# Two feed-forward networks by seven products: a fourth pair in the down panels, x kept in DRAM, its blocks added by accumulating DMAs

## The chip, the core and the metric

The kernel runs on one core of one Trainium2 chip, as one program. Its time is the device time of one execution, in microseconds; the median of three runs before the change is 2627.86 us (2625.54 to 2630.56). Five engines work side by side, each through its own list of instructions in a fixed order, and wait for each other at semaphores: TensorE (PE) multiplies, VectorE (DVE) and ScalarE (ACT) do the arithmetic on elements, GpSimd (POOL) and SyncE (SP) here mostly start DMAs.

## What is computed

Two transformer layers on 256 tokens of width 2048 in float32, each a mixer (state space or gated delta rule beside sparse attention) and a feed-forward network. The change touches the feed-forward networks and what hands x to them. Each is, after an RMS norm whose row factor is applied later,

```
u = rmsnorm(x, g_mlp) @ w_up          # [256, 2048] @ [2048, 8192]
x = x + jnp.square(jax.nn.relu(u)) @ w_down   # [256, 8192] @ [8192, 2048]
```

## The kernel before

Every number is split in two parts, hi (`whi`, `xnh`, `hTh`) and lo (`wlo`, `xnl`, `hTl`), and a product of two blocks is three matmuls: hi by hi, hi by lo, lo by hi. ACT copies a stretch of weights to `whi` (line 266 in the wide panels, 207 in the others), and DVE subtracts it from the weights for `wlo` (lines 267, 208). These have four buffers of 1024 columns each; a buffer is free again when PE has used it.

A network (`ffn`) goes in four steps (`s_`) of 2048 hidden columns. A step is four wide panels, called here U0 and U1 (two up panels, which make the hidden block) and D0 and D1 (two down panels, which add to x). A wide panel multiplies 256 tokens by 2048 rows and 1024 columns of weights; it goes through eight pairs, `j` from 0 to 7, of 256 rows. A pair is a 2 by 2 block problem: two token blocks, two halves of the rows, two halves of the columns. A plain pair takes eight products, 24 matmuls. For the pairs in `SPAIRS`, 2, 4 and 6, a seven-product scheme is used, 21 matmuls. It wants sums of the weight blocks, `t13` (line 284) and `t24` (287 and 288, after `t13`), all on DVE, then four splits: `w11` with `w22` straight from the weights, `t13`, `t24`, and a half one of the last block. It also wants sums of the activations, made once per pair (`a_forms`, lines 232 to 235, and a split, `sfh` on ACT and `sfl` on DVE).

After a wide panel, `shared` combines four banks of the accumulators (ACT copies P1 at 311, DVE adds at 312 to 315). After an up panel each of the four results gets its own bank added (DVE, 381), then ReLU and square on ACT (382, 383), then 16 transposes on PE (395), then a split to `hTh` and `hTl` (170, 172), and the sums for the pairs in `SPAIRS`, through a tile `ff`. All this is done while the next wide panel runs. After a down panel, the four results and the four banks are added to x in SBUF by eight DVE instructions (415, 418). The last down panel of a network is done by `panel` (plain products, lines 192 to 194).

The weights come in through SP's queue, 1 MB per pair, into three buffers `wst`; a load is started when DVE has made the last split of the pair three before. Large tiles share pools: seven `sp` (four of them hold x during a network, so three are left for `t13` and `t24`), seventeen `s4`, sixteen `s2`. The order of each engine's instructions is fixed at build time by a list scheduler, which goes by its own estimate of when things are ready and which prefers what stands earlier in the program.

Of the kernel before, what the change touches and what calls it, by code (L numbers as in the profile page):

```python
# [57 lines left out]
def build(ctx, tc, I, out, tap=None, upto=99):  # L58
# [162 lines left out]
    SPAIRS = (2, 4, 6)  # L221
    turn = [0]

    def two_forms():
        f = s4([128, 2, 512], name="ff")
        return f[:, 0].rearrange("p (k t c) -> p k t c", k=2, t=2), f[:, 1].rearrange("p (f c) -> p f c", f=4)
# [13 lines left out]
    def wide(w, r0, c0, lhs, forms):  # L240
# [8 lines left out]
        ns = len(SPAIRS)  # L249
# [20 lines left out]
        for j in range(8):  # L270
# [3 lines left out]
            if j not in SPAIRS:  # L274
                for kk in range(2):
                    xh, xl = lhs(2 * j + kk)
                    wl = parts(s[:, kk * 1024:(kk + 1) * 1024])[::-1]
                    for i, l, b in ((0, 0, "P2"), (0, 1, "P3"), (1, 0, "P4"), (1, 1, "E")):
                        h = slice(i * 128, i * 128 + 128)
                        product(b, xh[:, h], xl[:, h], *wl[l])  # L280
                continue
# [26 lines left out]
    def shared(B):  # L308

        p1, u2, u4, v = (s2([128, 512], name=n) for n in ("cp1", "cu2", "cu4", "cv"))  # L310
# [5 lines left out]
        return ((0, 0, p1, B["P2"]), (0, 1, u4, B["P3"]), (1, 0, u2, B["P4"]), (1, 1, v, B["E"]))  # L316
# [57 lines left out]
    def ffn(X, act, forms, w_up, w_down, r, after, tail=0):  # L374
        for s_ in range(4):
            hT, hforms = [], {}
            for P in range(2):
                B, tags = wide(w_up, 0, s_ * 2048 + P * 1024, at_k(act), forms)
                us = {}
                for i, l, part, bank in shared(B):  # L380
# [4 lines left out]
                for l in (1, 0):  # L385
# [3 lines left out]
                    for k0 in range(0, 4, 2):  # L389
# [7 lines left out]
                        if j in SPAIRS:  # L397
# [5 lines left out]
            for P in range(2):  # L403
                if (s_, P) == (3, 1):
# [7 lines left out]
                out_ = shared(B)  # L412
                for i, l, part, bank in out_:
                    x = X[2 * P + 1 - l][:, i]
                    V.tensor_tensor(x, part, x, op=OP.add)
                for i, l, part, bank in out_:
                    x = X[2 * P + 1 - l][:, i]
                    V.tensor_tensor(x, bank, x, op=OP.add)
                if s_ == 3:
                    for p in range(2):  # L420
# [369 lines left out]
    def add_panel(ps, p, scale, act, gain, ssx, forms):  # L790
# [5 lines left out]
        for t in range(2):  # L796
            sumsq(ssx[:, t, p:p + 1], X[p][:, t])

    X = x_panels()
# [20 lines left out]
    ffn(X, xn, xforms, I["w_up"][0], I["w_down"][0], r, after1)  # L820
# [513 lines left out]
    xforms = {}  # L1334
    ssx = tiny([128, 2, 4], "ssx", bufs=2)
    for p in range(4):
# [6 lines left out]
        for t in range(2):  # L1343
            sumsq(ssx[:, t, p:p + 1], X[p][:, t])
    r = x_rstd(ssx, "r4")
# [27 lines left out]
    ffn(X, xn, xforms, I["w_up_2"][0], I["w_down_2"][0], r, after2, tail=8)  # L1373
# [23 lines left out]
```

## Time and profile before

| | |
|---|---|
| median of 3 runs | 2627.86 us |
| profiled execution, whole | 2628.55 us |
| its span, first to last instruction | 2626.7 us |
| PE busy | 2600.1 us, 99% |
| weight loads of PE (PEld) busy | 2173.6 us, 83% |
| DVE busy | 2037.6 us, 78% |
| ACT busy | 1466.7 us, 56% |
| DMA | 478.64 MB, 182 GB/s |

The profile is one execution; times in it are microseconds from the span's start. Busy time is the union of an engine's instructions. A DVE or ACT instruction runs on a little after the next has begun, so in a row of instructions the price of one is the distance of two starts, a little less than its duration. A line such as L267 is a line of the kernel before; in the changed kernel it is the same line up to 286, and one to eleven later further down.

### The profile page before, as it was taken

Reading aid. Unit: us, or ns where it says so; the run is one execution under the profiler, and the core shown is the slowest. Engines: PE = TensorE matmul, PEld = TensorE weight load, DVE = VectorE, ACT = ScalarE, POOL = GpSimd, SP = SyncE. Lnnn points to the kernel's source line nnn. Section 1 sums busy time; section 2 is a strip of 40 time slices with the busy share of each in tenths; the row PEclk is TensorE's granted clock in tenths of the full one; section 3 lists DMA queues with packets and bytes.
Section 4 is the critical chain, followed back from the end, with each engine's and each line's share of the span. In section 5 each row is a group of like instructions: output and inputs, shape, how many; then the busy total and the mean of one; then the engine's idle time right before and its main releaser. Section 6 shows DMA issues by size and latency. Waiting matters only on the chain.

```text
span 2626.7 us, 32683 instructions
## 1 busy us (share of the span) xinstructions
PE 2600.1 (99%) x12566; PEld 2173.6 (83%) x12566; DVE 2037.6 (78%) x2797; ACT 1466.7 (56%) x1962; POOL 37.5 (1%) x46
## 2 busy tenths in 40 slices
PE   8999999999999999999999999999999999999998
PEld 8998888888888888888888887888888888888886
DVE  5767768998989999676755867455579999999996
ACT  5465456646657566554533655444457566565664
POOL 0000000000000000000000000000000000000000
PEclk9999999999999999999999999999999999999999
DMA  7454555565655655653432743556555655555654
GB/s 239 143 177 155 170 192 192 177 207 193 193 198 187 208 193 196 203 189 129 132 98 87 260 165 111 180 189 211 197 176 179 218 196 197 193 204 192 208 181 172
DMA packets 192154, 478.64 MB, mean 182 GB/s; under 512 B 9127, under 2 KB 50046, under 8 KB 191998
## 3 DMA queue, kind: packets, MB, share of 16 engines
q1 hardware_dynamic: 185840, 467.57, 53.7%
q10 hardware_dynamic: 6158, 8.99, 1.1%
q8 instruction: 98, 1.61, 0.2%
q14 instruction: 58, 0.48, 0.1%
HBM read 472.32 MB, written 4.21 MB: 181 GB/s over the span
## 4 chain that ended last, share of the span: by engine, by line
PE 90%; DVE 6%; DMA 2%; ACT 1%; issue 1%; ACTq 0%; POOL 0%; POOLq 0%; SPq 0%; DVEq 0%
PE mm L255 20%; PE mm L194 13%; PE mm L193 13%; PE mm L192 13%; PE tp L255 10%; PE sx L255 9%; DVE wlo L267 3%; DMA wst<-in_w_down_dram 1%; PE sx L987 1%; PE sx L982 1%; PE tp L350 1%; ACT whi L266 1%; PE mm L395 1%; PE tp L881 0%; PE sx L1266 0%
## 5 line engine op out<-in xcount | busy, mean ns | idle before, releaser
L208 DVE TENSOR_TENSOR wlo<-wst,whi 128x1024 fp32r<-128x1024 f32 (+6 forms) x416 | 475.5, 1146 | 318.2 <-ACT whi L207 316.3
L207 ACT ACTIVATE whi<-wst 128x1024 fp32r<-128x1024 f32 (+6 forms) x416 | 414.2, 998 | 442.0 <-PE mm L194 418.6
L266 ACT ACTIVATE whi<-wst 128x1024 fp32r<-128x1024 f32 x480 | 465.9, 979 | 274.5 <-PE mm L255 115.4
L267 DVE TENSOR_TENSOR wlo<-wst,whi 128x1024 fp32r<-128x1024 f32 x480 | 528.0, 1119 | 57.5 <-ACT whi L266 55.2
L266 ACT ACTIVATE whi<-t 128x1024 fp32r<-128x1024 f32 x180 | 190.3, 1057 | 214.9 <-DVE t L288 96.6
L194 PE MATMUL mm<-whi,x2l 128*128 128x512 f32 (+3 forms) x736 | 279.7, 380 | 0.0
L193 PE MATMUL mm<-wlo,x2h 128*128 128x512 f32 (+3 forms) x736 | 278.0, 378 | 0.9 <-DVE wlo L208 0.9
L192 PE MATMUL mm<-whi,x2h 128*128 128x512 f32 (+3 forms) x736 | 278.5, 379 | 0.0
L267 DVE TENSOR_TENSOR wlo<-t,whi 128x1024 fp32r<-128x1024 f32 x180 | 219.8, 1221 | 41.6 <-ACT whi L266 39.6
L193 PEld LDWEIGHTS mm<-wlo,x2h 128*128 128x128 f32 x736 | 138.7, 189 | 21.3 <-DVE wlo L208 1.3
L194 PEld LDWEIGHTS mm<-whi,x2l 128*128 128x128 f32 x736 | 138.5, 188 | 20.2 <-issue 1.0
L192 PEld LDWEIGHTS mm<-whi,x2h 128*128 128x128 f32 x736 | 138.7, 189 | 20.0 <-issue 0.8
L192 PE MATMUL mm<-whi,xnh 128*128 128x512 f32 (+3 forms) x416 | 152.7, 368 | 2.0 <-ACT whi L207 1.6
L255 PE MATMUL mm<-wlo,xnh 128*128 128x512 f32 x392 | 152.9, 390 | 0.0
L255 PE MATMUL mm<-whi,xnl 128*128 128x512 f32 x392 | 152.7, 389 | 0.0
L255 PE MATMUL mm<-whi,xnh 128*128 128x512 f32 x392 | 151.9, 391 | 0.7 <-ACT whi L266 0.7
L193 PE MATMUL mm<-wlo,xnh 128*128 128x512 f32 (+3 forms) x416 | 151.9, 365 | 0.0
L194 PE MATMUL mm<-whi,xnl 128*128 128x512 f32 (+3 forms) x416 | 150.7, 365 | 0.0
L255 PE MATMUL mm<-wlo,hTh 128*128 128x512 f32 x343 | 134.0, 391 | 0.0
L255 PE MATMUL mm<-whi,hTl 128*128 128x512 f32 x343 | 133.6, 390 | 0.0
L255 PE MATMUL mm<-whi,hTh 128*128 128x512 f32 x343 | 132.1, 391 | 0.0
L284 DVE TENSOR_TENSOR t<-wst 128x1024 f32<-128x1024 f32 x90 | 109.8, 1220 | 13.7 <-DMA wst<-in_w_down_dram 11.2
(534 smaller groups left out, 5414.7 us busy)
## 6 DMA issues: line engine op xcount, KB each, us to landing
wst<-in_w_up_dram SPq DMA_DIRECT2D x128, 1024.0 KB, 5.0
wst<-in_w_down_dram SPq DMA_DIRECT2D x128, 1024.0 KB, 5.4
wst<-in_w_in_dram SPq DMA_DIRECT2D x84, 1024.0 KB, 5.1
wst<-in_w_out_dram SPq DMA_DIRECT2D x16, 1024.0 KB, 5.1
wst<-in_w_o_dram SPq DMA_DIRECT2D x16, 1024.0 KB, 5.0
wst<-in_w_in_dram SPq DMA_DIRECT2D x16, 780.0 KB, 4.4
wst<-in_w_in_dram SPq DMA_DIRECT2D x12, 824.0 KB, 4.5
wst<-in_w_in_dram SPq DMA_DIRECT2D x12, 736.0 KB, 6.2
```

Of the source, the lines that this page charges most:

```text
L192: PE.matmul(ps[t][:, :n], xh[:, sl], wa, start=kt == first, stop=False)
L193: PE.matmul(ps[t][:, :n], xh[:, sl], wb, start=False, stop=False)
L194: PE.matmul(ps[t][:, :n], xl[:, sl], wa, start=False, stop=kt == last)
L207: S.activation(a[:, :2 * n], src, AF.Copy)
L208: V.tensor_tensor(b[:, :2 * n], src, a[:, :2 * n].bitcast(F32), op=OP.subtract)
L255: PE.matmul(B[b], x, y, start=left[b] == total[b], stop=left[b] == 1)
L266: S.activation(a[:, :n], src, AF.Copy)
L267: V.tensor_tensor(b[:, :n], src, a[:, :n].bitcast(F32), op=OP.subtract)
L284: V.tensor_tensor(t13, s.rearrange("p (k l n) -> p k l n", k=2, l=2)[:, :, 0], s[:, :1024].rearrange("p (l n) -> p l n", l=2)[:, ::-1], op ...
L350: PE.transpose(ps[:, kk, t, :], x[:, t, (k0 + kk) * 128:(k0 + kk + 1) * 128], ident)
L395: PE.transpose(pv[:, kk, t, :], us[t, l][:, c:c + 128], ident)
L982: PE.matmul(ps[:, i * 64:(i + 1) * 64].rearrange("p (m b) -> p m b", b=b), N[:, i], half(T[:, i], 0), start=True, stop=True)
```

## The change

The pairs of the down panels that go by seven products become 2, 3, 5 and 6 (`DPAIRS`); the up panels keep 2, 4 and 6. To make room, x leaves SBUF: each panel of x is written to a DRAM tile `xd` by a DMA of ACT's queue when it is complete, before a network starts. In steps 0 to 2 the blocks of a down panel are finished in the tiles `ca` and `cb` (their own bank added to each, four DVE instructions where there were eight), and each of the two tiles is added to `xd` by an accumulating DMA of POOL's queue. In step 3 the panels of x are loaded back by ACT's queue, two before D0 and two before the last panel, and the blocks are added to them by DVE. The four results of `shared` lie now in `ca` (an `sp` tile) and `cb` (an `s4` tile) instead of four `s2` tiles, and `ff` is an `sp` tile.

```
-    SPAIRS = (2, 4, 6)
+    SPAIRS, DPAIRS = (2, 4, 6), (2, 3, 5, 6)
...
     def two_forms():
-        f = s4([128, 2, 512], name="ff")
+        f = sp([128, 2, 512], name="ff")
...
-        ns = len(SPAIRS)
+        ns = len(forms)
...
-            if j not in SPAIRS:
+            if j not in forms:
...
     def shared(B):
-        p1, u2, u4, v = (s2([128, 512], name=n) for n in ("cp1", "cu2", "cu4", "cv"))
+        ca, cb = sp([128, 2, 512], name="ca"), s4([128, 2, 512], name="cb")
+        p1, u2, u4, v = ca[:, 0], ca[:, 1], cb[:, 0], cb[:, 1]
         S.activation(p1, B["P1"], AF.Copy)
         V.tensor_tensor(u2, B["P6"], p1, op=OP.add)
         V.tensor_tensor(u4, B["P5"], u2, op=OP.add)
         V.tensor_tensor(u2, B["P7"], u2, op=OP.add)
         V.tensor_tensor(v, B["P5"], u2, op=OP.add)
-        return ((0, 0, p1, B["P2"]), (0, 1, u4, B["P3"]), (1, 0, u2, B["P4"]), (1, 1, v, B["E"]))
+        return ((0, 0, p1, B["P2"]), (0, 1, u4, B["P3"]), (1, 0, u2, B["P4"]), (1, 1, v, B["E"])), (ca, cb)
...
-    def ffn(X, act, forms, w_up, w_down, r, after, tail=0):
+    def ffn(act, forms, xd, w_up, w_down, r, after, tail=0):
...
-                for i, l, part, bank in shared(B):
+                for i, l, part, bank in shared(B)[0]:
                     V.tensor_tensor(part, bank, part, op=OP.add)
...
-                        if j in SPAIRS:
+                        if j in DPAIRS:
                             f = two_forms()
                             S.activation(f[0].rearrange("p k t c -> p (k t c)"), pt, AF.Copy)
                             f_to_act(f, q, k0, hforms, j)
...
             for P in range(2):
+                if s_ == 3:
+                    for p in (2 * P, 2 * P + 1):
+                        X[p] = sp([128, 2, 512], name=f"X{p}")
+                        nc.scalar.dma_start(X[p], xd[:, p])
                 if (s_, P) == (3, 1):
...
                 B, _ = wide(w_down, s_ * 2048, P * 1024, at_k(hT), hforms)
-                out_ = shared(B)
+                out_, pair = shared(B)
                 for i, l, part, bank in out_:
-                    x = X[2 * P + 1 - l][:, i]
-                    V.tensor_tensor(x, part, x, op=OP.add)
-                for i, l, part, bank in out_:
-                    x = X[2 * P + 1 - l][:, i]
-                    V.tensor_tensor(x, bank, x, op=OP.add)
-                if s_ == 3:
-                    for p in range(2):
+                    V.tensor_tensor(part, bank, part, op=OP.add)
+                    if s_ == 3:
+                        x = X[2 * P + 1 - l][:, i]
+                        V.tensor_tensor(x, part, x, op=OP.add)
+                for l in (1, 0):
+                    p = 2 * P + 1 - l
+                    if s_ < 3:
+                        G.dma_start(xd[:, p], pair[l], accum_op=OP.add)
+                    else:
                         for t in range(2):
                             after(p, t)
...
             sumsq(ssx[:, t, p:p + 1], X[p][:, t])
-
+        nc.scalar.dma_start(xd[:, p], X[p])
+
+    xd = drp.tile([128, 4, 2, 512], F32, name="xd")
...
+        nc.scalar.dma_start(xd2[:, p], X[p])
```

The order of the instructions moves at three places that repeat in each step.

The first is DVE in D0, from the last bank addition of U1 (`cv` before, `cb` now, not shown) to the last split of pair 2; `t` with a number is `t13` or `t24`. Before:

```order
L267 TENSOR_TENSOR wlo<-wst,whi 128x1024 x2
L284 TENSOR_TENSOR t_5906<-wst 128x1024
L287 TENSOR_TENSOR t_5908<-wst,t_5906 128x512
L288 TENSOR_TENSOR t_5908<-wst,t_5908 128x512
L267 TENSOR_TENSOR wlo<-wst,whi 128x1024
L232 TENSOR_TENSOR ff<-ff 128x128
...
L267 TENSOR_TENSOR wlo<-t_5906,whi 128x1024
...
L172 TENSOR_TENSOR sfl<-ff,sfh 128x512
L267 TENSOR_TENSOR wlo<-t_5908,whi 128x1024
L267 TENSOR_TENSOR wlo<-wst,whi 128x512
L267 TENSOR_TENSOR wlo<-wst,whi 128x1024 x2
```

and now, where `t_5935` and `t_5937` are pair 2's, and `t_5979` is pair 3's `t13`:

```order
L267 TENSOR_TENSOR wlo<-wst,whi 128x1024 x3
L172 TENSOR_TENSOR hTl<-tp,hTh 128x512
...
L172 TENSOR_TENSOR hTl<-sx,hTh 128x512
L172 TENSOR_TENSOR sfl<-ff,sfh 128x512
...
L284 TENSOR_TENSOR t_5935<-wst 128x1024
L172 TENSOR_TENSOR sfl<-ff,sfh 128x512
L287 TENSOR_TENSOR t_5937<-wst,t_5935 128x512
L267 TENSOR_TENSOR wlo<-t_5935,whi 128x1024
L288 TENSOR_TENSOR t_5937<-wst,t_5937 128x512
L284 TENSOR_TENSOR t_5979<-wst 128x1024
L267 TENSOR_TENSOR wlo<-t_5937,whi 128x1024
L267 TENSOR_TENSOR wlo<-wst,whi 128x512
```

What moved: the three instructions of `t13` and `t24` of pair 2 stood between the second and the third split of weights and stand now behind the work on `hTl` and `ff`; and pair 3's `t13` stands before the split of pair 2's `t24`.

The second is DVE in U1, from the last bank addition of U0 on. Before:

```order
L267 TENSOR_TENSOR wlo<-wst,whi 128x1024 x2
L284 TENSOR_TENSOR t_5523<-wst 128x1024
L287 TENSOR_TENSOR t_5525<-wst,t_5523 128x512
L288 TENSOR_TENSOR t_5525<-wst,t_5525 128x512
L267 TENSOR_TENSOR wlo<-wst,whi 128x1024
L172 TENSOR_TENSOR hTl<-mm_5405,hTh 128x512
...
L267 TENSOR_TENSOR wlo<-t_5523,whi 128x1024
L172 TENSOR_TENSOR sfl<-ff,sfh 128x512
L267 TENSOR_TENSOR wlo<-t_5525,whi 128x1024
L267 TENSOR_TENSOR wlo<-wst,whi 128x512
```

and now, where `t_5632` is pair 4's `t13`:

```order
L267 TENSOR_TENSOR wlo<-wst,whi 128x1024 x3
L172 TENSOR_TENSOR hTl<-mm_5426,hTh 128x512
...
L172 TENSOR_TENSOR hTl<-ff,hTh 128x512
...
L234 TENSOR_TENSOR ff<-ff 128x128
L284 TENSOR_TENSOR t_5554<-wst 128x1024
L172 TENSOR_TENSOR sfl<-ff,sfh 128x512
...
L287 TENSOR_TENSOR t_5556<-wst,t_5554 128x512
L267 TENSOR_TENSOR wlo<-t_5554,whi 128x1024
L172 TENSOR_TENSOR sfl<-ff,sfh 128x512
L288 TENSOR_TENSOR t_5556<-wst,t_5556 128x512
L284 TENSOR_TENSOR t_5632<-wst 128x1024
L267 TENSOR_TENSOR wlo<-t_5556,whi 128x1024
```

The same moved here, and there are two sets of activation sums (eight instructions on `ff`, two `sfl`) instead of one, since pairs 2 and 3 of the down panels want them both.

The third is PE in D0, pair 2. A product is a matmul with `whi`, one with `wlo` and again one with `whi`; `wlo_5922` before and `wlo_5951` now is the lo part of `t13`, `wlo_5932` and `wlo_5961` that of `t24`. Before:

```order
L255 MATMUL tp_5833<-whi_5921,sfh_5434 128x512
L255 MATMUL tp_5833<-wlo_5922,sfh_5434 128x512
L255 MATMUL tp_5833<-whi_5921,sfl_5435 128x512
L255 MATMUL sx_5835<-whi_5921,sfh_5434 128x512
L255 MATMUL sx_5835<-wlo_5922,sfh_5434 128x512
L255 MATMUL sx_5835<-whi_5921,sfl_5435 128x512
L255 MATMUL sx_5834<-whi_5931,sfh_5434 128x512
L255 MATMUL mm1_5830<-whi_5931,hTh_5419 128x512
L255 MATMUL sx_5834<-wlo_5932,sfh_5434 128x512
L255 MATMUL sx_5834<-whi_5931,sfl_5435 128x512
L255 MATMUL mm1_5830<-wlo_5932,hTh_5419 128x512
```

and now:

```order
L255 MATMUL tp_5862<-whi_5950,sfh_5455 128x512
L255 MATMUL sx_5864<-whi_5950,sfh_5455 128x512
L255 MATMUL tp_5862<-wlo_5951,sfh_5455 128x512
L255 MATMUL tp_5862<-whi_5950,sfl_5456 128x512
L255 MATMUL sx_5864<-wlo_5951,sfh_5455 128x512
L255 MATMUL sx_5864<-whi_5950,sfl_5456 128x512
L255 MATMUL sx_5863<-whi_5960,sfh_5455 128x512
L255 MATMUL mm1_5859<-whi_5960,hTh_5440 128x512
L255 MATMUL mm0_5857<-whi_5970,hTh_5440 128x512
L255 MATMUL sx_5863<-wlo_5961,sfh_5455 128x512
L255 MATMUL sx_5863<-whi_5960,sfl_5456 128x512
L255 MATMUL mm1_5859<-wlo_5961,hTh_5440 128x512
```

More of the products' first matmuls, which want `whi` alone, stand ahead of the first matmul with a `wlo`.

## Rows read from the trace of the kernel before

**Rows 1.** The profile's page: the span, and each engine's busy time

```profile
span 2626.7 us, 32683 instructions
...
PE 2600.1 (99%) x12566; PEld 2173.6 (83%) x12566; DVE 2037.6 (78%) x2797; ACT 1466.7 (56%) x1962; POOL 37.5 (1%) x46
```

**Rows 2.** Busy time by engine, then clock and DMA, in one 100 us stretch

```profile
800.00:900.00 100.00, 99.89 (x451) 82.22 (x450) 92.88 (x115) 62.86 (x76) 0.00 (x0) 1.00 0.57 184
```

**Rows 3.** Waits of PE: who waited for whom, total us, times, longest

```profile
PE mm L192 <- DVE X L418: 2.6, 1, 2.6
...
PE tp L255 <- DVE wlo L267: 1.4, 3, 0.6
```

**Rows 4.** The chain that ended last: start, us, what

```profile
716.15 5.39 DMA wst<-in_w_down_dram
...
799.39 1.47 PE mm L395 x12
...
949.00 6.80 PE mm L255 x30
...
971.23 1.47 PE mm L395 x12
...
2193.12 1.47 PE mm L395 x12
...
2363.72 1.47 PE mm L395 x12
```

**Rows 5.** Timeline of DVE in D0: start us, us, engine, line, what

```profile
838.67 0.68 DVE L381 TENSOR_TENSOR cv<-sx,cv 128x512 f32<-128x512 f32 x1
839.26 2.35 DVE L267 TENSOR_TENSOR wlo<-wst,whi 128x1024 fp32r<-128x1024 f32 x2
841.53 1.22 DVE L284 TENSOR_TENSOR t<-wst 128x1024 f32<-128x1024 f32 x1
...
844.26 1.23 DVE L267 TENSOR_TENSOR wlo<-wst,whi 128x1024 fp32r<-128x1024 f32 x1
...
847.55 0.28 DVE L232 TENSOR_TENSOR ff<-ff 128x128 f32<-128x128 f32 x1
847.75 0.28 DVE L233 TENSOR_TENSOR ff<-ff 128x128 f32<-128x128 f32 x1
...
850.70 0.68 DVE L172 TENSOR_TENSOR hTl<-sx,hTh 128x512 fp32r<-128x512 f32 x1
851.30 0.68 DVE L172 TENSOR_TENSOR sfl<-ff,sfh 128x512 fp32r<-128x512 f32 x1
851.90 1.22 DVE L267 TENSOR_TENSOR wlo<-t,whi 128x1024 fp32r<-128x1024 f32 x1
```

**Rows 6.** Timeline of ACT in D0

```profile
843.18 1.04 ACT L266 ACTIVATE whi<-wst 128x1024 fp32r<-128x1024 f32 x1
844.13 0.57 ACT L399 ACTIVATE ff<-tp 128x512 f32<-128x512 f32 x1
```

**Rows 7.** Timeline of PE in D0: its first product, and its first need

```profile
837.48 0.39 PE L255 MATMUL mm<-whi,hTh 128*128 128x512 f32 x1
...
853.53 0.39 PE L255 MATMUL sx<-wlo,sfh 128*128 128x512 f32 x1
```

**Rows 8.** Timeline of DVE in U1

```profile
806.93 1.22 DVE L267 TENSOR_TENSOR wlo<-t,whi 128x1024 fp32r<-128x1024 f32 x1
```

**Rows 9.** Timeline of PE in U1

```profile
809.82 0.39 PE L255 MATMUL mm<-wlo,sfh 128*128 128x512 f32 x1
```

**Rows 10.** Timeline of PE behind the last D0 of the second network

```profile
2572.33 0.39 PE L192 MATMUL mm<-whi,hTh 128*128 128x512 f32 x1
```

**Rows 11.** DMAs: issue, queue, count, KB each, median us to landing

```profile
wst<-in_w_down_dram SPq DMA_DIRECT2D x128, 1024.0 KB, 5.4
...
xsave<-X ACTq DMA_DIRECT2D x4, 512.0 KB, 5.9
```

**Rows 12.** The DMA of one tile: time of an issue, ns, min/median/max

```profile
L818 ACTq DMA_DIRECT2D xsave<-X x4: 326/336/353, 1056.6 to 1105.9; - x4
```

More of the change, by code (lines that the diff above doesn't have):

```diff
@@ L818, in after1 @@
             nc.scalar.dma_start(xsave[:, p], X[p])
-    ffn(X, xn, xforms, I["w_up"][0], I["w_down"][0], r, after1)
+    ffn(xn, xforms, xd, I["w_up"][0], I["w_down"][0], r, after1)
     if upto == 2:
@@ L1334, in build @@
     xforms = {}
+    xd2 = drp.tile([128, 4, 2, 512], F32, name="xd2")
     ssx = tiny([128, 2, 4], "ssx", bufs=2)
@@ L1371, in after2 @@
         nc.sync.dma_start(o[:, 1024:1536], X[2][:, t])
-    ffn(X, xn, xforms, I["w_up_2"][0], I["w_down_2"][0], r, after2, tail=8)
+    ffn(xn, xforms, xd2, I["w_up_2"][0], I["w_down_2"][0], r, after2, tail=8)
 _INS = ["x", "g_mix", "w_in", "conv_w", "conv_b", "dt_bias", "a_log", "d_skip", "g_ssd", "g_q", "g_k", "g_kidx",
```

## The prediction

> **What bounds the kernel now.** I read the page first: PE is busy for 2600.1 of 2626.7 us [rows 1], so fewer matmuls ought to be less time. Then a stretch of 100 us inside a feed-forward network: PE 99.89, but DVE 92.88 [rows 2], against 78% over the whole span. In the networks DVE is close behind PE. The list of PE's waits is short; one for x behind the first network's last D0, and a few for `wlo`, 1.4 us in all, show who would be late first [rows 3]. The chain gives prices for PE: 30 matmuls take 6.80 us, 0.227 each; the transposes of U1 come back after 171.84 us in the first network (799.39 to 971.23) and after 170.60 in the second (2193.12 to 2363.72), so a step of the first network holds 1.24 us of waiting, which the chain puts into D1, behind DVE and a load of weights [rows 4].
>
> DVE's timeline gives its prices as distances of starts: a split or sum of 1024 columns 1.13 us (two take 2.35, one 1.22), one of 512 columns 0.60 (850.70 to 851.30), one of 128 columns 0.20 (847.55 to 847.75) [rows 5]. A plain pair costs DVE 2 x 1.13 = 2.27 and PE 24 x 0.227 = 5.44. A pair by seven products costs DVE 1.13 + 2 x 0.60 for `t13` and `t24` and 3 x 1.13 + 0.60 for the splits, 6.32 together, and PE 21 x 0.227 = 4.76. So in a seven-product pair DVE is the slower, and lives on the lead that it wins in plain pairs.
>
> **What goes.** Each wide down panel loses one product of three matmuls. There are 14 of them (four steps with two, less the last, in two networks), 42 matmuls, 42 x 0.227 = **9.5 us** of PE. Four of the eight additions to x behind a down panel go in steps 0 to 2, 2.4 us of DVE each time, at the place where the first network's chain runs through DVE into a load. I take these waits as gone, 3 x 1.24 = **3.7 us**; they could also stay, so 0 to 3.7.
>
> **What DVE gets.** A step gets 2 x (6.32 - 2.27) = 8.1 us for the pairs and 4 x 0.20 + 0.60 = 1.4 for one more set of activation sums, less 8 x 0.60 = 4.8 for the additions: 4.7 us in 170, while it idles for 7 in 100 [rows 2]. By the sum there is room. What decides is where in the panel it falls, and the order tells that.
>
> **D0.** Count from PE's first product at 837.48 [rows 7]. Before, DVE ended U1's bank additions with the one begun at 838.67, made two splits from 839.26 on, then at 841.53 `t13` and `t24`, and at 844.26 the third split [rows 5]. ACT, which has eight ReLU and square instructions to do first, began that split's `whi` only at 843.18 and went on to the next at 844.13 [rows 6]. So the sums, 1.13 + 2 x 0.60 = 2.33 us, filled a gap of 2.73 in which DVE had nothing else. Now the third split follows the second at once; it still cannot begin before about 844.26, DVE stands still for the 2.7 us, and the 2.33 of the sums come behind, after the work on `hTl` and `ff` (as much of it as before). Pair 3's `t13`, 1.13, is now also ahead of the split of pair 2's `t24`. That split began at 851.90 and is done 1.22 later, at 853.12; PE wanted it at 853.53 [rows 5, 7], 0.41 to spare. It will be 2.33 + 1.13 - 0.41 = 3.05 late. PE has one more matmul that needs no `wlo` ahead of this point, so it loses 3.05 - 0.23 = 2.8. Pair 3 follows by seven products: from that split to the same one of pair 3 DVE needs 1.13 + 0.60 + 0.60 + 1.13 + 0.60 + 1.13 = 5.2 us, and PE has 20 matmuls, 4.5 us, so 0.65 more. **3.45 us a panel, eight times: 27.6.** Pair 4 is plain and DVE wins 5.44 - 2.27 = 3.2 there, which pairs 5 and 6 use up (2 x 1.56). I cost them at nothing, covered by pair 4; uncovered they are 1.5 a panel.
>
> **U1.** The same three instructions move behind `hTl` and `ff`, pair 4's `t13` is put before the split of pair 2's `t24`, and there is the second set of activation sums: 2.33 + 1.13 + 1.4 = 4.86. That split was done at 806.93 + 1.22 = 808.15 [rows 8] and wanted at 809.82 [rows 9], 1.67 to spare: 3.2 late. Two matmuls move ahead, 0.45. **2.75 a panel, eight times: 22.0.** Pair 3 is plain here, and DVE regains its lead. U0 and D1 have no `hTl` work, and lose four or no additions; I cost them at nothing.
>
> **Queues.** POOL gets 24 accumulating DMAs of 512 KB. No row shows one. Nearest are a store of 512 KB, 5.9 us to landing, and a load of weights, 5.4 [rows 11]. Nothing but the reuse of `ca` and `cb` waits for them, a panel (40 us) later, and POOL has nothing behind them that is due. They can only slow the loads. A load is asked for when a pair is split and used when two more are, a plain and a seven-product one, 2.27 + 6.32 = 8.6 us later, so it has 3.2 us to spare. From below the price is nothing; if each pair of DMAs holds up one load by the 5.9 us of a store, 2.7 us come through twelve times, 32 us. I take nothing, since the store's row is below the 8.6, and keep the 32. ACT starts 16 DMAs more, 0.34 us each [rows 12]: eight beside panels bound by PE, four in front of the last panel of a network, four in D0's work of step 3, where they could cost PE up to 0.7 twice. I take nothing, as ACT is ahead of DVE there.
>
> **Behind the last D0** PE waited 2.6 us for x in the first network [rows 3] and went straight on in the second [rows 10]. Now the next panel's first splits stand behind all bank additions, whose last needs the end of D0: one addition, one addition to x and one split, some 2 us in either network. 4.1 against 2.6: **1.5 us**, between 0 and 4.
>
> **The sum** goes against the execution profiled, 2628.55 us (0.7 above the median): 2628.55 - 9.5 - 3.7 + 27.6 + 22.0 + 1.5 = 2666.5, so **2666 us**. The two large terms are differences of starts and spare times that were read to 0.01 us; what is open in them is whether ACT, whose `whi` of a sum follows that sum, adds its own latency of about 1 us (1.04 in [rows 6]) at the new places, and how much PE regains by the order of its matmuls. I give each panel -1.5 to +1: 2642 to 2682.
>
> **Rivals.** (1) The lead covers it, PE stays the bound and the time is 2628.55 - 9.5 - 3.7 = 2615, faster. For it: DVE's idle 7%, PE's 99%, and that the sums need nothing that is late. It decides at ACT: if its `whi` of the third split were there before 842, DVE would not stand still and 2.33 of the loss would go in each panel. Against: ACT began it at 843.18, behind work that the change leaves as it is. The Trainium skill (Perfetto Trace Analysis, Identifying the Most-Contended Engine) speaks for this rival: it takes the engine with the highest occupancy as the one to work on, with weight loads instead of matmuls for TensorE. By weight loads, 82.22, DVE is the most contended here already, and with 4.7 us more a step it would stand at 96%, still below full, so by that rule nothing comes of it but the gain of PE. The trace agrees on DVE's place; that occupancy below 100% means no loss it does not bear out, as DVE with 92.88 has only 0.41 us to spare in D0. (2) Only one of the two places loses, because PE's order or ACT gives the other back: 2666 - 25 = 2641. (3) The accumulating DMAs slow the loads as priced: 2666 + 32 = 2698; waits for `wst` in D1 and U0 would show it. (4) The products don't go, since `wide` might still count three pairs: the built order has 42 matmuls less on PE, so I give this no chance.
>
> **How the numbers follow.** Forecast 0.70; rival 1 0.11; rival 2 0.08; rival 3 0.08; 0.03 for a loss that just pays for the gain. A measurement of this kernel tells 0.2%, 5 us, from no change: faster 0.11, same 0.03, slower 0.86. The range reaches from rival 2 to half way to rival 3 and leaves out rival 1 and the far end: 2640 to 2686.
>
> **What will show it.** PE's waits for `wlo` of L267 and the `whi` ahead of it grow from some 2 us to some 50, eight times 2 to 3 us in U1 and eight times 3 to 4 us in D0, all in pairs 2 and 3; a step takes about 175 us instead of 170.6. DVE stands idle for 2.7 us before the third split of weights, waiting for ACT. If PE shows no such waits, or they stand at pairs 5 and 6, the account of the order is wrong; if it waits for `wst`, that of the queues is.

## The result and the profile after

The changed kernel takes 2707.86 us (2706.11 to 2708.65, four runs) against 2629.05 us before on the same chip: a ratio of 1.0298 [1.0286, 1.031], slower by 79 us where 38 were forecast. The direction was right; the time lies outside the range.

The page of the changed kernel, its span and busy times, answers to [rows 1]:

```profile
span 2706.9 us, 32847 instructions
...
PE 2628.2 (97%) x12524; PEld 2168.0 (80%) x12524; DVE 2077.5 (77%) x2859; ACT 1494.0 (55%) x2006; POOL 59.0 (2%) x70
```

PE has the 42 matmuls fewer (12566 to 12524), and the span is 80 us longer. No engine but POOL is busier in share than it was. What has grown is the list of PE's waits, which answers to [rows 3] (who waited for whom, total us, times, longest):

```profile
PE mm L255 <- DVE wlo L267: 14.3, 18, 2.9
PE mm L255 <- ACT whi L266: 11.0, 15, 1.2
PE tp L255 <- DVE wlo L267: 10.8, 11, 2.4
PE sx L255 <- ACT whi L266: 9.8, 12, 1.2
PE mm L193 <- DVE wlo L208: 9.1, 3, 6.4
```

To see where they fall, measure each panel on PE, from its first matmul with a `wlo` to the end of its last with a `wlo`, and compare the sums over both networks. D0's forecast is 27.6 less eight times 0.68 for its products, D1's the 3.7 and six times 0.68.

| | before, each | after, each | forecast, all | measured, all |
|---|---|---|---|---|
| U0 behind a step (6), and first of a network (2) | 41.7 (42.2, 42.5) | 43.2 to 45.9 (42.2, 42.4) | 0 | +17.1 |
| U1 (8) | 43.2 | 46.4 to 47.3 | +22.0 | +27.5 |
| D0 (8) | 43.2 | 47.2 | +22.2 | +32.1 |
| D1 (6) | 41.3 to 42.6 | 40.6 | -7.8 | -7.7 |
| behind the two last D0 | | | +1.5 | +2.9 and +7.5 |

With 0.8 at the start that is 80.2 us, the difference of the two spans.

**D0** is where the forecast worked in detail. DVE's timeline, which answers to [rows 5]; the last column is the idle time before a row and who ended it:

```profile
862.13 2.35 DVE L267 TENSOR_TENSOR wlo<-wst,whi 128x1024 fp32r<-128x1024 f32 x2
867.07 1.23 DVE L267 TENSOR_TENSOR wlo<-wst,whi 128x1024 fp32r<-128x1024 f32 x1 [2.59 <-ACT whi L266]
...
872.86 1.22 DVE L284 TENSOR_TENSOR t<-wst 128x1024 f32<-128x1024 f32 x1
...
877.01 1.22 DVE L284 TENSOR_TENSOR t<-wst 128x1024 f32<-128x1024 f32 x1
878.27 1.22 DVE L267 TENSOR_TENSOR wlo<-t,whi 128x1024 fp32r<-128x1024 f32 x1
```

DVE stands still for 2.59 us before the third split (2.7 forecast), and the split of pair 2's `t24` begins 17.98 us after PE's first product at 860.29; by the forecast, 14.42 + 2.33 + 1.13 = 17.88. PE's rows, which answer to [rows 7]:

```profile
860.29 0.39 PE L255 MATMUL mm<-whi,hTh 128*128 128x512 f32 x1
...
875.28 0.50 PE L255 MATMUL tp<-whi,sfh 128*128 128x512 f32 x1 [0.59 <-ACT whi L266]
875.62 0.40 PE L255 MATMUL sx<-whi,sfh 128*128 128x512 f32 x1
876.54 0.50 PE L255 MATMUL tp<-wlo,sfh 128*128 128x512 f32 x1 [0.53 <-DVE wlo L267]
...
878.29 0.50 PE L255 MATMUL sx<-whi,sfh 128*128 128x512 f32 x1 [0.56 <-ACT whi L266]
...
879.55 0.50 PE L255 MATMUL sx<-wlo,sfh 128*128 128x512 f32 x1 [0.24 <-DVE wlo L267]
...
883.67 0.50 PE L255 MATMUL sx<-whi,sfh 128*128 128x512 f32 x1 [0.59 <-ACT whi L266]
```

PE does not stop once for `wlo`, as the sum has it, but at four places of pair 2 and one of pair 3, three of the five for ACT.

In **U1** pair 2 shows the same, PE's rows answering to [rows 9]:

```profile
829.31 0.50 PE L255 MATMUL mm<-wlo,sfh 128*128 128x512 f32 x1 [0.65 <-DVE wlo L267]
...
831.67 0.50 PE L255 MATMUL mm<-whi,sfh 128*128 128x512 f32 x1 [1.16 <-ACT whi L266]
...
832.93 0.50 PE L255 MATMUL mm<-wlo,sfh 128*128 128x512 f32 x1 [0.24 <-DVE wlo L267]
```

**U0**, which the forecast left out. DVE there before, pair 3's first split and then pair 4's `t13`:

```profile
766.09 1.23 DVE L267 TENSOR_TENSOR wlo<-wst,whi 128x1024 fp32r<-128x1024 f32 x1 [0.48 <-ACT whi L266]
767.23 1.22 DVE L284 TENSOR_TENSOR t<-wst 128x1024 f32<-128x1024 f32 x1
```

and now, with `t13` ahead of that split, then PE and the loads:

```profile
779.90 0.69 DVE L267 TENSOR_TENSOR wlo<-wst,whi 128x512 fp32r<-128x512 f32 x1
783.85 1.23 DVE L284 TENSOR_TENSOR t<-wst 128x1024 f32<-128x1024 f32 x1 [3.25 <-DMA wst<-in_w_up_dram]
784.99 1.22 DVE L267 TENSOR_TENSOR wlo<-wst,whi 128x1024 fp32r<-128x1024 f32 x1
```

```profile
786.26 0.50 PE L255 MATMUL mm<-wlo,xnh 128*128 128x512 f32 x1 [2.14 <-DVE wlo L267]
...
787.14 0.63 PE L255 MATMUL mm<-wlo,xnh 128*128 128x512 f32 x1
787.57 0.63 PE L255 MATMUL mm<-whi,xnl 128*128 128x512 f32 x1
```

```profile
wst<-in_w_up_dram SPq DMA_DIRECT2D x4, 1024.0 KB, 10.9
xd<-ca POOLq DMA_DIRECT2D x1, 512.0 KB, 6.5
xd<-cb POOLq DMA_DIRECT2D x1, 512.0 KB, 10.4
```

The last three are the DMAs started in U0's first 22 us, with their median time from issue to landing (of the loads, the two whose landing the trace tells). While two accumulating DMAs are in flight, these loads take 10.9 us; in the same stretch before, the one that is told took 6.1. Pair 4's `t13` at 783.85 waits 3.25 us for such a load, and pair 3's split, whose weights are long there, stands behind it in DVE's order; PE waits for that split. It is so in all six U0 behind a step: DVE waits 2.8 to 4.0 us for the load, and PE 1.7 to 2.9 for DVE.

**Behind the last D0** of the second network, where [rows 10] had PE go straight on, PE and DVE:

```profile
2644.94 0.61 PE L192 MATMUL mm<-whi,hTh 128*128 128x512 f32 x2
2651.93 0.79 PE L193 MATMUL mm<-wlo,hTh 128*128 128x512 f32 x1 [6.38 <-DVE wlo L208]
```

```profile
2649.45 0.69 DVE L1369 TENSOR_TENSOR X<-X,lnf 128x512 f32<-128x512 f32 x1 [1.46 <-ACT junk L167]
2650.06 0.68 DVE L422 TENSOR_TENSOR X<-cb,X 128x512 f32<-128x512 f32 x1
2650.66 1.22 DVE L208 TENSOR_TENSOR wlo<-wst,whi 128x1024 fp32r<-128x1024 f32 x1
```

Behind the end of D0 (2645) there stand, ahead of the next panel's first split, not the two additions that were forecast but two bank additions, three additions to x and a multiplication by the norm's weights that itself waits for ACT.

### The profile page after: what moved, and what is told of

It is laid out like the page before. It is cut to its first block, busy times and chain, and to the rows that moved or that the text cites. A ratio compares the mean times of both kernels' runs of the same rounds, so it can differ in the third digit from the quotient of the medians.

```text
span 2706.9 us, 32847 instructions
## 1 busy us (share of the span) xinstructions
PE 2628.2 (97%) x12524; PEld 2168.0 (80%) x12524; DVE 2077.5 (77%) x2859; ACT 1494.0 (55%) x2006; POOL 59.0 (2%) x70
## 4 chain that ended last, share of the span: by engine, by line
PE 80%; DVE 10%; ACT 6%; DMA 3%; issue 1%; POOL 0%; ACTq 0%; POOLq 0%; SPq 0%; DVEq 0%
PE mm L255 17%; PE mm L194 13%; PE mm L193 13%; PE mm L192 13%; PE tp L255 8%; PE sx L255 8%; DVE wlo L267 4%; ACT whi L266 3%; DMA wst<-in_w_up_dram 2%; DVE hTl L172 1%; DVE t L284 1%; ACT ca L383 1%; PE sx L996 1%; ACT cb L383 1%; PE sx L991 1%
## 5 line engine op out<-in xcount | busy, mean ns | idle before, releaser
L267 DVE TENSOR_TENSOR wlo<-wst,whi 128x1024 fp32r<-128x1024 f32 x480 | 521.0, 1104 | 92.2 <-ACT whi L266 90.1
L266 ACT ACTIVATE whi<-wst 128x1024 fp32r<-128x1024 f32 x480 | 452.5, 963 | 239.0 <-PE mm L255 88.9
L266 ACT ACTIVATE whi<-t 128x1024 fp32r<-128x1024 f32 x208 | 220.0, 1058 | 251.0 <-DVE t L288 100.4
L267 DVE TENSOR_TENSOR wlo<-t,whi 128x1024 fp32r<-128x1024 f32 x208 | 253.9, 1222 | 27.7 <-ACT whi L266 22.7
L284 DVE TENSOR_TENSOR t<-wst 128x1024 f32<-128x1024 f32 x104 | 126.9, 1220 | 26.9 <-DMA wst<-in_w_up_dram 26.7
L255 PE MATMUL mm<-wlo,hTh 128*128 128x512 f32 x308 | 121.0, 393 | 0.0
L255 PE MATMUL mm<-whi,hTl 128*128 128x512 f32 x308 | 120.1, 390 | 0.0
L255 PE MATMUL mm<-whi,hTh 128*128 128x512 f32 x308 | 118.6, 391 | 0.0
```

The lines of the kernel that those rows point to most:

```text
L255: PE.matmul(B[b], x, y, start=left[b] == total[b], stop=left[b] == 1)
L266: S.activation(a[:, :n], src, AF.Copy)
L267: V.tensor_tensor(b[:, :n], src, a[:, :n].bitcast(F32), op=OP.subtract)
L284: V.tensor_tensor(t13, s.rearrange("p (k l n) -> p k l n", k=2, l=2)[:, :, 0], s[:, :1024].rearrange("p (l n) -> p l n", l=2)[:, ::-1], op ...
```

## The experiments

"Order" is the theory that DVE's order makes the loss, "pairs" that the fourth pair does, "queues" that the accumulating DMAs do. All ratios are against the kernel before, in the same rounds.

**Which part moves the order?** One edit in the kernel before:

```
-        f = s4([128, 2, 512], name="ff")
+        f = sp([128, 2, 512], name="ff")
```

> The kernel before with one edit: the tile ff lies in the sp tiles instead of the s4 tiles. x stays in SBUF, three pairs, no accumulating DMA. The three sums t13 and t24 of pair 2 then stand behind the work on hTl and ff on VectorE, in U1 and in D0, as in the changed kernel. Theory 'order' (the loss in U1 and D0 comes from where ff lies, since t13 and ff then draw from the same tiles in turn): D0 2.33 + 1.13 of sums late, less 0.41 and one matmul to spare, plus restarts of PE, about 3.1 a panel; U1 2.33 + 1.13 less 1.67 and two matmuls, plus restarts, about 1.9 a panel; eight of each, 40 us: 2669 us (2655 to 2680). Rival 'pairs' (the loss comes from VectorE's work for the fourth pair and the neighbouring pairs 2 and 3): within 5 us of the kernel before, 2629.

Measured: 2669.49 us, 1.0152 [1.0137, 1.0167]. Three pairs, x in SBUF, not one matmul fewer, and 40 us lost: U1 45.0 to 45.8, D0 46.3 to 47.4; that is 15.5 us more in all eight U1 (27.5 in the changed kernel) and 29.4 in all D0 (32.1). DVE's rows in D0 are those of the changed kernel, the third split behind the same wait, and `t13` 10.7 us behind the first splits (852.85) instead of 2.3:

```profile
857.79 1.23 DVE L267 TENSOR_TENSOR wlo<-wst,whi 128x1024 fp32r<-128x1024 f32 x1 [2.59 <-ACT whi L266]
...
863.54 1.23 DVE L284 TENSOR_TENSOR t<-wst 128x1024 f32<-128x1024 f32 x1
```

So the loss in U1 and D0 is mostly not the fourth pair's. It comes with `ff` drawing from the same `sp` tiles as `t13`; whether the turn in which the tiles are handed out does it or their number, no run parts. The converse, in the changed kernel:

```
-        f = sp([128, 2, 512], name="ff")
-        return f[:, 0].rearrange(...), f[:, 1].rearrange(...)
+        f, sf = s2([128, 512], name="ff"), s2([128, 512], name="fs")
+        return f.rearrange(...), sf.rearrange(...)
```

> The changed kernel with one edit: ff is two s2 tiles of 512 columns, so that t13 and t24 no longer follow it. In U1 the three sums of pair 2 stand ahead of the third split again, in D0 two of the three, with pair 3's t13 in the gap as well. Theory 'order': U1 comes back from 46.5 to about 43.4 us (-25), D0 from 47.2 to about 43.3 (-31), U0 and the stretch behind the last D0 stay as they are: 2708 - 56 = 2652 us (2640 to 2668). Rival 'pairs': U1 and D0 stay within 1 us a panel of the changed kernel, 2695 to 2708.

Measured: 2657.47 us, 1.0105 [1.009, 1.012]; U1 43.3 to 43.7, D0 44.8 (the last ones 47.4 and 46.2), U0 43.0 to 44.0. 50 of the 79 us come back, 25 of them in U1 and 14.5 in D0, the rest in U0 and between the networks. In D0 the second half of `t24` still stands behind the first work on `hTl`, and D0 stays some 1.7 above the 43.2 of before, with three matmuls less.

**The DMAs.** The changed kernel without them (x then lacks the blocks of steps 0 to 2):

```
-                    if s_ < 3:
-                        G.dma_start(xd[:, p], pair[l], accum_op=OP.add)
-                    else:
+                    if s_ == 3:
```

> The changed kernel without its 24 accumulating DMAs: the blocks of the steps 0 to 2 are not added to x. VectorE's order inside the networks is the same as with them. Theory 'queues' (they slow the weight loads of U0, and PE then waits at pair 3): the six U0 behind another step fall from 43.2 to 45.9 to about 42, 17 us, U1 and D0 stay: 2691 us (2686 to 2696). Rival 'order in U0' (pair 4's t13, which stands ahead of pair 3's splits, is late by itself): U0 stays, 2703 to 2708.

Measured: 2689.83 us, 1.0224 [1.0207, 1.0241]; U0 41.2 to 41.8, the loads of that stretch 5.4 us. And as plain stores:

```
-                        G.dma_start(xd[:, p], pair[l], accum_op=OP.add)
+                        G.dma_start(xd[:, p], pair[l])
```

> The changed kernel with its 24 accumulating DMAs turned into plain stores to the same places (x then loses what was in it). VectorE's order is the same. Theory 'accumulating' (it is the adding that slows the loads of weights, the DMA reading what it adds to): U0 41.2 as without any DMA, 2690 us (2684 to 2695). Rival 'traffic' (any 1 MB written at the start of U0 slows them): U0 stays at 43 to 46, 2700 to 2708.

Measured: 2688.24 us, 1.0225 [1.0211, 1.0239]; U0 41.2. A store and the loads beside it, same stretch:

```profile
wst<-in_w_up_dram SPq DMA_DIRECT2D x5, 1024.0 KB, 6.7
xd<-cb POOLq DMA_DIRECT2D x1, 512.0 KB, 6.2
```

It is the adding that costs. POOL's queue (packets, MB, share of the 16 DMA engines' time) in the 22 us of the changed kernel, and in those of the plain stores:

```profile
q0 software_dynamic: 288, 1.05, 31.4%
...
q0 software_dynamic: 288, 1.05, 13.4%
```

The same packets and bytes hold the DMA engines more than twice as long. Then the order of U0 alone, in the changed kernel with all its DMAs; `done` is the list of DVE's splits in the panel, and `issue_after` fixes the order without a wait:

```
+            with tc.issue_after(done[-2]) if first and j > 2 else nullcontext():
                 V.tensor_tensor(t13, ...)
...
-                B, tags = wide(w_up, 0, s_ * 2048 + P * 1024, at_k(act), forms)
+                B, tags = wide(w_up, 0, s_ * 2048 + P * 1024, at_k(act), forms, P == 0)
```

> The changed kernel with one edit: in U0, the t13 of pairs 4 and 6 comes behind the first split of the plain pair ahead of it. The accumulating DMAs, ff in the sp tiles and the order of U1, D0 and D1 stay. Theory 'queues times order' (a slowed load is a loss in U0 only because pair 4's t13, which waits for it, stands ahead of pair 3's splits): U0 from 43.2 to 45.9 down to 41.2 us, with the load as late as it was: 2708 - 20 = 2688 us (2684 to 2693). Rival 'queues alone' (the slowed loads hold up U0 in any order): 2700 to 2708.

Measured: 2689.67 us, 1.0225 [1.021, 1.024], as if there were no DMAs; U0 41.2 to 41.3, while the loads still take 10.8. The load and DVE at the place:

```profile
wst<-in_w_up_dram SPq DMA_DIRECT2D x5, 1024.0 KB, 10.8
```

```profile
777.46 1.23 DVE L270 TENSOR_TENSOR wlo<-wst,whi 128x1024 fp32r<-128x1024 f32 x1 [1.80 <-ACT whi L269]
778.85 1.23 DVE L288 TENSOR_TENSOR t<-wst 128x1024 f32<-128x1024 f32 x1 [0.15 <-DMA wst<-in_w_up_dram]
```

Pair 3's split now goes first, and `t13` waits 0.15 us instead of 3.25. The loss of U0 needs both: the slowed load, and an instruction that waits for it ahead of one that is due.

**Behind the last D0**, in the changed kernel: the additions to x of D0 and their `after` are written behind the call of `panel`, and POOL's queue loads x:

```
-                        nc.scalar.dma_start(X[p], xd[:, p])
+                        G.dma_start(X[p], xd[:, p])
...
                         ps = panel(w_down, s_ * 2048, 16, p * 512, 512, at_k(hT), tail=tail if p == 3 else 0)
+                        if p == 2:
+                            for i, l, part, bank in late:
+                                x = X[1 - l][:, i]
+                                V.tensor_tensor(x, part, x, op=OP.add)
+                            for q in range(2):
+                                for t in range(2):
+                                    after(q, t)
```

> The changed kernel with one edit, in step 3 alone: behind the last D0 the additions to x come after the next panel's first part in the program, so that VectorE makes that panel's splits first, and x is loaded back by POOL's queue instead of ACT's. Theory 'order': the second network's last panels from 62.0 us to some 54.5, and 1 to 3 us behind the first network: 2708 - 9 = 2699 us (2695 to 2703). Rival (the panel waits for x or its banks, not for its splits): 2705 to 2709 us.

Measured: 2694.27 us, 1.0241 [1.0223, 1.0259], 13.6 less than the changed kernel and a little more gain than expected: the end 9.3 shorter (52.7 us from the last D0), the stretch between the networks 4.1. The 6.38 us are gone. The two edits were not separated.

**What the parts of the change are worth.** The changed kernel with `ff` in `s2` and

```
-    SPAIRS, DPAIRS = (2, 4, 6), (2, 3, 5, 6)
+    SPAIRS, DPAIRS = (2, 4, 6), (2, 4, 6)
```

> The changed kernel with three pairs (2, 4, 6) in the down panels, as before the change, and ff in two s2 tiles: what is left of the change is x in DRAM with its accumulating DMAs. The sums of pair 2 stand ahead of the work on hTl and ff. In U0 pair 4's t13, which wants a load of weights, stands ahead of the last split of pair 2. Theory 'queues' (a slowed load is a loss wherever a t13 that waits for it stands ahead of work that is due): U1 and D0 as before (43.2), the six U0 behind another step 3 us longer (41.7 to about 45), D1 0.6 shorter, 8 us behind the last D0: 2629 + 18 - 3 + 8 = 2652 us (2640 to 2662). Rival 'pairs' (x in DRAM is free, the fourth pair costs): 2625 to 2635.

Measured: 2684.76 us, 1.0214 [1.0199, 1.0229], 33 more than expected. U0 44.5 to 45.7 as expected, but D1 too, 45.0 to 45.9 where 41.3 to 42.6 were before: here pair 4's `t13` stands ahead of a split that is due in D1 as well, and DVE waits 47.1 us in all for loads of the down weights. The mechanism is that of U0; that it would reach D1 was not foreseen. Then four pairs with x in SBUF, the kernel before with `ff` in `s2` and

```
+    SPAIRS, DPAIRS = (2, 4, 6), (2, 3, 5, 6)
...
+        ca, cb = sp([128, 2, 512], name="ca"), s4([128, 2, 512], name="cb")
```

> Four pairs by seven products in the down panels, but x stays in SBUF as before (eight additions to x, no DMA of x): the four results of shared lie in ca and cb, and ff is two s2 tiles. The sums of pair 2 stand ahead of the work on hTl and ff in U1 and D0. Theory 'order and queues' (nothing but these two made the changed kernel slow): U0 and U1 as before, D1 and D0 less the products (-0.68 each), D0 with 1.5 to 2 us more at pair 3, which follows pair 2 at once: 2629 - 9.5 + 8 x 1.5 = 2631 us (2620 to 2643). Rival 'pairs' (VectorE has no room for the fourth pair; with the additions to x its share in a step is some 98%): 2670 or more.

Measured: 2673.11 us, 1.0161 [1.0146, 1.0176]: the expectation failed, by 42 us, and the time lies where the rival "pairs" had it. D0 takes 44.7 to 45.5, and behind each of the six D1 PE stands some 3.5 us, since DVE makes the eight additions to x first and only then goes on with U0's splits. D0 makes 15 us of the loss and these stops 21; whether D0's share is the fourth pair's or its order's this run does not tell.

**Mending the order.** With `ff` in `s2`: in U1 and D0 the fourth split behind pair 2's `t24`; each later `t13` behind a split of the pair before; behind the last D0 the additions as above, with x still loaded by ACT's queue.

```
+            with tc.issue_after(done[-2]) if j > 2 else nullcontext():
                 V.tensor_tensor(t13, ...)
...
+            if early and j == 2:
+                tc.add_manual_dep(done[3], t24b.ins.name, ...)   # order alone
```

> The kernel of the experiment with ff in s2 (four pairs, x in DRAM), and VectorE's order pinned at four places: pair 2's t13 and t24 ahead of the fourth split of weights in U1 and D0, a later pair's t13 behind the first split of a plain pair before it or the t24 split of a seven-product pair before it, and behind the last D0 the next panel's splits ahead of the additions to x. Theory 'order': D0 from 44.8 to about 42.8 us (-16), the last D0 of each network from 47.4 to 43 (-8), U0 from 43.5 to 42.5 (-6), behind the last D0 -7: 2655 - 37 = 2618 us (2610 to 2632), faster than the kernel before. Rival 'pairs' (VectorE is full at pairs 2 and 3 in whatever order): D0 stays above 44, 2640 or more.

Measured: 2675.73 us, 1.0183 [1.0168, 1.0198]. U0 came to 41.2 to 41.6, but D1 went from 40.6 to 44.2, D0 to 46.8 and the last ones to 52.2: what was pinned was worse than what the scheduler had. The time is again in the range of "pairs". Four weight tiles change little of that:

```
-    stp = ctx.enter_context(tc.tile_pool(name="stp", bufs=3))
+    stp = ctx.enter_context(tc.tile_pool(name="stp", bufs=4))
-    NP, N4, N2, N1 = 7, 17, 16, 5
+    NP, N4, N2, N1 = 6, 16, 16, 5
...
-        ca, cb = sp([128, 2, 512], name="ca"), s4([128, 2, 512], name="cb")
+        ca, cb = sp([128, 2, 512], name="ca"), sp([128, 2, 512], name="cb")
```

> The kernel with the mended order, and four weight tiles (wst) instead of three, so that each load of weights is asked for one pair earlier; the room comes from one sp and one s4 tile less, and cb is an sp tile. The accumulating DMAs stay. Theory 'queues' (they cost only because a load has some 3 us to spare): U0 falls to about 41.2 us as without them, some 8 us less than with three tiles: 2610 us (2602 to 2618). Rival: the load is not what U0 waits for, or the missing sp and s4 tiles cost as much elsewhere: the same as with three tiles or slower.

Measured: 2677.66 us, 1.0189 [1.0174, 1.0205], as the rival has it; U0 41.2, D1 44.2. The last D0 fall to some 48.2, but the first network starts 9.5 us later than in the run before. Nor does x in SBUF help, with the additions in the next panel (`mid` is called ahead of pair 5):

```
-                        G.dma_start(xd[:, 2 * P + 1 - l], pair[l], accum_op=OP.add)
+                late += [(X[2 * P + 1 - l][:, i], part) for i, l, part, bank in out_]
...
+    MID = 5
...
+            if j == MID and mid:
+                mid()
```

> The kernel with the mended order, but x stays in SBUF: no accumulating DMA, and the four additions to x of a down panel come in the next panel, from its pair 5 on, instead of at the panel's end. VectorE gets 2.4 us more in each U0 and D1 than with x in DRAM. Theory 'order and queues': U0 41.7 us as before, U1 43.2, D0 42.6, D1 41 (its additions stand among the seven-product pairs): 2629 - 9.5 - 4 + 3 = 2618 us (2610 to 2628). Rival 'pairs' (VectorE is full): D1 above 42.5 and U0 above 42.5, 2632 or more.

Measured: 2665.83 us, 1.0143 [1.0126, 1.0159]; U0 41.2, as the theory has it, but D0 46.8 and D1 44.1, as "pairs" has it.

So a later `t13` is pinned only behind a plain pair, the fourth split behind pair 2's `t24` in D0 alone, POOL's queue loads x, and D0 goes back to three pairs, two of them neighbours that come late. The four were changed together:

```
+    D0 = (2, 5, 6)
-            with tc.issue_after(done[-2]) if j > 2 else nullcontext():
+            with tc.issue_after(done[-2]) if j > 2 and j - 1 not in forms else nullcontext():
...
+                B, _ = wide(..., {j: f for j, f in hforms.items() if P or j in D0}, P == 0)
```

> x in DRAM with its accumulating DMAs, ff in two s2 tiles, four pairs (2, 3, 5, 6) by seven products in D1 alone; D0 takes three of them (2, 5, 6), with its pair 3 plain. VectorE's order: pair 2's t13 and t24 ahead of the fourth split of weights in D0; a t13 behind a plain pair comes after that pair's first split, a t13 behind a seven-product pair is left where the scheduler puts it (ahead of the t24 split of the pair before). Behind the last D0 the next panel's splits come ahead of the additions to x; x is loaded back by POOL's queue instead of ACT's. Theory 'lead' (four pairs fit where the panel does not begin with the work on hTl and ff, that is in D1, and there an early t13 of the next pair fills the time in which VectorE waits for ScalarE): U0 41.2, U1 43.4, D0 43.3, D1 40.6 us: 168.5 a step against some 170.5 and 169.4 before; 2629 - 11 - 3 = 2615 us (2608 to 2624). Rival 'pairs' (the fourth pair costs wherever it is): D1 above 42, 2630 or more.

Measured: 2613.52 us (2612.88 to 2614.13), 0.9941 [0.9928, 0.9955], faster than both. U0 41.2, U1 43.4, D0 43.2, D1 40.5. So the fourth pair does not cost wherever it is; that it costs in D0 stays possible, since no run with four pairs there came below 44.7. The longest of PE's waits, among which no wide panel is left:

```profile
PE tp L142 <- DMA P<-in_g_mix_dram: 5.5, 1, 5.5
PE mm L193 <- ACT whi L208: 1.6, 1, 1.6
PE mm L194 <- DVE wlo L209: 1.3, 1, 1.3
```

The same with x in SBUF and the additions in the next panel (`late` and `mid`, as above):

> The kernel with four pairs in D1 alone, but x stays in SBUF: no DMA of x, and the four additions to x of a down panel come in the next panel from pair 5 on (2.4 us of VectorE in each U0 and each D1). Theory 'lead' (VectorE has no lead to give in D1, where four pairs go by seven products): U0 41.2, D1 from 40.6 to 41.5 or 42.5 us, 6 to 12 us: 2620 to 2626, x in DRAM is worth about that. Rival: the additions fall into time in which VectorE waits for ScalarE, and x in DRAM is worth nothing: 2611 to 2617 us.

Measured: 2619.56 us, 0.9961 [0.9948, 0.9973]: D1 41.3, so x in DRAM is worth some 6 us, the least that the theory gave. Last, what had made D1 longer in the mended order. First the place of `t13` (`and j - 1 not in forms` taken out again):

> The kernel with four pairs in D1 alone and one edit: a t13 whose pair follows a seven-product pair comes behind the t24 split of that pair, not ahead of it. Theory 'fill' (ahead of the split it costs nothing, since VectorE waits there for ScalarE's whi of t24; behind it, pair 3 and pair 6 begin their chain later): D1 from 40.6 to 44.2 us, D0 up to 1 us longer at pair 6: 2613 + 22 + 4 = 2638 us (2630 to 2645). Rival, as in the prediction (a t13 ahead of the split makes that split 1.13 us later): the same or faster, 2606 to 2614 us.

Measured: 2613.48 us, 0.9942 [0.9927, 0.9957], the same: the theory "fill" is wrong. The rival has this time in its range, but the 1.13 us that the split should gain by it do not show. Then the second half of `t24`:

```
+            if j - 1 in forms:
+                tc.add_manual_dep(t24b.ins, done[-1].name, ...)   # behind the split of t13
```

> The kernel with four pairs in D1 alone and one edit: in a pair that follows a seven-product pair (3 and 6 in D1, 6 in D0) the second half of t24 comes behind the split of t13 instead of ahead of it. Theory 'chain' (that split waits for ScalarE's whi of t13, so t24 is complete later, ScalarE's whi of t24 too, and the split of t24 waits for that; this made D1 44.2 us in the kernels with the mended order): D1 from 40.6 to some 44 us, D0 up to 1 us longer: 2613 + 20 + 4 = 2637 us (2628 to 2645). Rival (the place of this one instruction does not matter, VectorE having slack there): 2611 to 2617 us.

Measured: 2630.41 us, 1.0002 [0.9993, 1.0011]; D1 42.3, D0 43.6 to 43.9. The chain is real:

```profile
724.94 1.22 DVE L271 TENSOR_TENSOR wlo<-t,whi 128x1024 fp32r<-128x1024 f32 x1
726.08 0.69 DVE L293 TENSOR_TENSOR t<-wst,t 128x512 f32<-128x512 f32 x1
727.98 1.23 DVE L271 TENSOR_TENSOR wlo<-t,whi 128x1024 fp32r<-128x1024 f32 x1 [1.21 <-ACT whi L270]
```

One instruction of 0.6 us put behind a split makes DVE wait 1.21 us for ACT. It explains 1.8 of the 3.6 us of D1; where the rest of the mended order's loss comes from stays open.

## Why the prediction was right in sign and wrong in size

**What bounds.** That DVE's place in the panel decides, not its share, holds. The Trainium skill (Perfetto Trace Analysis, Identifying the Most-Contended Engine) takes the engine with the highest occupancy as the one to optimize first; that room below 100% makes a loss impossible was rival 1's reading of it. Occupancy did not tell this loss: with `ff` moved DVE is busy for 2039.9 us against 2037.6 before, and the kernel takes 40 us more.

**Products, D1.** Right: -7.7 against -7.8, the waits of the first network's D1 gone with the products.

**D0 and U1.** The mechanism was right, and the experiment with `ff` alone in the kernel before shows it. The terms "3.45 us a panel" and "2.75 a panel" were mis-sized. In D0 PE's stops and restarts come to 4.5 us more than before: 3.1 in pair 2 (2.8 forecast), 0.9 at pair 3 (0.65), 0.5 at pairs 5 and 6, which "cost them at nothing, covered by pair 4" left out. In U1 pair 2's stops come to 3.1, and in two of the eight panels the clock falls and they take 47.2 and 47.3. What the sum missed in pair 2 is that one late split becomes four stops in D0 and three in U1, each with a restart; two of the four and one of the three are for ACT's `whi` of a sum, which the prediction named as open. With `ff` moved in the kernel before, pair 2's stops in D0 come to 3.1 as well. The sign that was named, waits of "some 50" us, came out at 49.7, but by luck: 13.6 of them are U0's, where none were forecast.

**Queues: "I take nothing".** This step failed, with 17.1 us (some 20, counted from the 41.2 that U0 takes, without the additions to x, when nothing holds it up). It set the 5.9 us of a store against 8.6, but an accumulating DMA is not a store: the loads beside it took 10.9 us. The Trainium skill (DMA: Bandwidth & Descriptors, Rules for kernel authors) says that an accumulate reads its destination and writes it later. The runs agree as far as they go: stores of the same bytes leave U0 at 41.2; no row shows the reading. But the loads alone would not have cost it: the forecast read DVE's order in U1 and D0 and put U0 "at nothing" without reading it there, where pair 4's `t13` had moved ahead of pair 3's splits: a fourth place, beside the three whose order is shown with the change. Rival 3 named D1 and U0; in D1 the loads were slow too (11.1 to 11.8 us in the first network) and PE did not wait, as the order there was another. The sign given for it, PE waiting for `wst`, did not show either: DVE waits for the load, and PE for DVE.

**"Behind the last D0, 1.5 us"** failed the same way, with 10.4: the number of instructions ahead of the next split was taken from the diff and not from the order.

**Rivals 1 and 2** are out: U1 and D0 both lost. Of the 42 us by which the lengths exceed the forecast, U0 makes 17, D0 10, the last D0s 9 and U1 5.5. The range's upper end was also not what it was said to be: half way to rival 3 is 2682, not 2686.

## What to carry to other kernels

Tiles that share a pool can share an order: moving one tile to another pool can put an instruction that was early behind all that draws from that pool before it, so read the order of every stage after such an edit, those without new work too. An engine with a fixed order that waits for a transfer holds up what is due behind it, so put what waits longest behind what is ready. And put extra work of a nearly full engine into the stage where it has a lead: four pairs paid in D1, and in none of the orders tried in D0.

## What was not expected of the hardware

An accumulating DMA of 512 KB landed after 7.5 us (`ca`) and 11.3 (`cb`, started right after), medians of twelve; as plain stores from the same queue 5.0 and 7.7.

After a stop PE restarts slowly: the first matmul takes 0.50 us and the next begins 0.34 behind it, instead of 0.39 and 0.23 (875.28 and 875.62 above). Behind some stops the clock falls as well. Stretches of U0 (us, PE busy and matmuls, granted clock, DMA share, GB/s):

```profile
784.00:786.00 2.00, 0.12 (x1) 1.00 0.53 199
786.00:788.00 2.00, 1.74 (x6) 0.74 0.09 33
788.00:790.00 2.00, 2.00 (x6) 0.50 0.52 98
790.00:792.00 2.00, 2.00 (x9) 0.91 0.98 395
...
2168.00:2170.00 2.00, 2.00 (x11) 1.00 0.47 70
```

Behind the stop of 2.14 us the granted clock is 0.50, the lower level, 1.2 GHz, and matmuls come every 0.43 us; eight of them cost some 1.6 us beyond the stop. It fell so behind all three stops of U0 in the first network (2.29, 2.14 and 2.86 us) and behind none of the second (2.37, 1.69 and 2.29; the last row above is behind the 2.37): a stop of 2.29 us made its U0 3.65 us longer in the first network and 2.05 in the second. So the length of the stop alone does not decide, and what does stays open; some 5 of U0's 17 us are the lower clock. Behind the 6.38 us at the end it was 0.50 from 2653 to 2656. Two stops of 0.65 and 1.16 us close to each other left it at 1.00 in one U1 (826 to 840), and in the first U1, with the same stops, the mean from 470 to 474 was 0.64.
